# Sample queries first, projections in quarter chunks, and prompt values in plain float32 on four column quarters

## The chip, the cores and the metric

The kernel runs on one core of one Trainium2 chip. The metric is the device time of one execution in microseconds. Three runs of the kernel before gave 2160.17, 2162.57 and 2163.04 us, a median of 2162.57 us. A separate execution was taken with the hardware profiler; its own time was 2163.56 us, of which its trace spans 2161.8 us.

## The reference, cut to what matters

One decoder layer is computed for 1024 prompt tokens and 32 sample tokens (8 sequences of 4 tokens with 2048 cached positions each), all in float32:

```
x = x + 0.5 * swiglu(rms_norm(x), w1, w3, w2)          # FFN 1
p = rms_norm(x) @ w_in                                  # q, k, v, forget logits, B gate, C gate, conv input
logf = log_sigmoid(fl + b_f);  uc = cg * u
o = softmax(q.k / 8 + sum of logf between key and query, causal) . v     # 8 heads of 64
      # prompt: 1024 keys of its own;  sample: 2048 cached keys by page table + its 4 new ones
conv = bg * conv3(uc)                                   # 512 channels, causal, width 3
x = x + concat(rms_norm(o), rms_norm(conv)) @ w_out
x = x + 0.5 * swiglu(rms_norm(x), w1', w3', w2')        # FFN 2
y = rms_norm(x)
```

Outputs are y for prompt and sample, and the new k, v, logf and conv state.

## The kernel before, in words

Activations stand with channels on the partitions and the 1056 tokens along the free side. A float32 product is mostly made of three matmuls in the rounded type `fp32r`: weight and activation are each split into a high and a low part (ScalarE casts the high part, line 86, VectorE subtracts for the low part, line 88), and `mm3` (lines 101 to 105) adds high x high, high x low and low x high. A few products (transposes, sample attention, some of the prompt's values) use plain float32 matmuls; the trace records each of these as two matmul instructions.

The order of instructions on each engine is not simply the order of the program. A planner goes over the whole program at compile time, with its own estimates of durations and with the program order as priority, and fixes an order for each engine and each DMA queue. On the chip every engine then runs its list strictly in order, and waits at an instruction whose input is late.

The stages in time are FFN 1 up and down (to about 741 us), the mixer (741 to 1147 us: all projections by `w_in`, and the whole attention of the sample tokens), the attention of the prompt (1147 to 1309 us), the output projection `w_out` (to about 1420 us), and FFN 2.

*Mixer, lines 570 to 982.* `w_in` is used in 24 column blocks of 128 (4 each of q, k, v, B gate, C gate, conv input). `proj`, `values` and `conv` load one block (512 KB, line 78, on SP's queue), split it, and compute it for three chunks of 352 tokens; `win` (line 612) makes one chunk, 8 x 3 matmuls, in one of three PSUM buffers `pg`. The prompt's q and k are written to memory as high and low parts (line 648), k also as an output (line 644), v twice (lines 961, 962); all of these go through SP's queue. `forget` (line 656) computes the forget gates and their running sums. The attention of the sample tokens, `sample(g)` for two groups of four sequences, is a generator. It first scans the cached forget gates (VectorE, line 823), which `load_gates` gathers page by page through the POOL queue (line 599; 16 gathers per group, by a table `idl` that 16 small DMAs of line 462 fill). Then it takes 16 chunks of keys (1 MB each: two pages on SP's queue, line 781, two on POOL's, line 599, into a ring of four buffers `kvraw`) for the scores (line 832), does the softmax, transposes it (line 859), and takes 16 chunks of values (line 874). Its products have 32 output rows per head pair, and use the array as four column quarters of 32 at the same time. In program order the four q blocks come first, whole; then k, values and conv run chunk by chunk, and after each chunk the sample generator is stepped at 1.2, 0.9 and 1.5 steps per chunk (lines 972 to 982).

*Attention of the prompt, lines 991 to 1128.* It runs over 8 heads x 8 query blocks of 128. `logits` computes scores (lines 1049, 1050, 1052), maximum, exponential and scaled probabilities `Pr`; it runs LA = 3 blocks ahead. `flip` transposes `Pr` by TensorE (line 1069) and copies it out of PSUM. `weigh` multiplies with the values for a pair of query blocks, PVD = 4 blocks behind. Even heads split probabilities and values into high and low parts: two `fp32r` matmuls of 256 columns per key block j (lines 1089, 1090), after a copy on ScalarE (line 1073) and a subtraction on VectorE (line 1075). Odd heads (`NATIVE`) use one plain float32 matmul of 64 rows by 256 columns per j (line 1085). A query block pair m needs 2m + 2 key blocks, of which the last has 128 columns: 20 per head. Two of the four chunks of the conv norm are placed after blocks 28 and 60 (`CONV_AT`). The loads of `w_out` are tied behind the loads of head 6 (`K.after`, line 1038).

Of the kernel before, what the change touches and what calls it, by code (L numbers as in the profile page):

```python
# [18 lines left out]
P = 128  # L19
# [8 lines left out]
H = 8  # L28
# [11 lines left out]
NATIVE = (1, 3, 5, 7)  # L40
LA, PVD, PTB, PRB = 3, 4, 3, 4
CONV_AT = (28, 60)
RK, RV, RC = 1.2, 0.9, 1.5
# [384 lines left out]
def kernel(ctx: ExitStack, tc: tile.TileContext, io: dict):  # L428
# [141 lines left out]
    with ExitStack() as es:  # L570
# [85 lines left out]
        def forget(other):  # L656
# [8 lines left out]
            for c in range(NMC):  # L665
                if c == NMC - 1:

                    other()
# [7 lines left out]
                nc.vector.tensor_add(z[:H, cs], ps[32:32 + H], z[:H, cs])  # L676
            zt = mix.tile([P, 9, H], F32, name="zt")
# [27 lines left out]
            nc.sync.dma_start(io["fo"][SEQ:TOK, :], lf[:NS, 8, :])  # L705
            LF = mix.tile([P, TOK], F32, tag="U", bufs=1, name="LF")
# [10 lines left out]
            T2 = smp.tile([P, PAST + P], F32, tag="B", bufs=1, name="T2")  # L717
# [19 lines left out]
            for t in range(1, NT):  # L737
# [3 lines left out]
                                  cst[:H, C_SELH:C_SELH + P].rearrange("h (b a c) -> h a b c", a=NHP, c=8))  # L741
            pcn = ptr.tile([P, 512], F32, tag="tr", name="pcn")[:, :NS]
# [45 lines left out]
        new = []  # L788
# [24 lines left out]
        def sample(g):  # L813

            if g == 0:
                load_gates(0)
            S = smp.tile([P, PAST + P], F32, tag="S", bufs=1, name="S")
            nc.gpsimd.memset(S[:, PAST + NS:], NEG)
            B = smp.tile([P, PAST + P], F32, tag="B", bufs=1, name="B")
            nc.vector.memset(B[:, 0:1], 0.0)  # L820
# [30 lines left out]
            if g == 0:  # L851
                load_gates(1)
# [11 lines left out]
            while not new:  # L864
                yield
# [469 lines left out]
```

## Time and profile before

| | us |
|---|---|
| runs, median of 3 | 2162.57 |
| profiled execution, its own time | 2163.56 |
| its span | 2161.8 |
| mixer stage, 741 to 1147 us | 406 |
| prompt attention, 1147 to 1309 us | 162 |

In the rows below, PE is TensorE's matmul, PEld its weight load, DVE is VectorE, ACT ScalarE, POOL GpSimd, SP SyncE (whose queue issues most DMAs). `L103` is line 103 of the kernel. A matmul's recorded duration overlaps the next matmul, so the time that one takes is read from start to start.

### The profile page before, as it was taken

What the parts mean: (1) busy time and instruction counts of PE and PEld (TensorE: products, weight loads), DVE (VectorE), ACT (ScalarE), POOL (GpSimd) and SP (SyncE); (2) the same over time, 40 slices, a digit from 0 to 9 for tenths busy, and PEclk for the clock granted to TensorE, in tenths of its full rate; (3) what the DMA queues carried; (4) which work ended last, traced back from release to release, by engine and by line L of the source; (5) the groups of instructions that cost most, each with busy time, mean ns of one, the idle gap of its engine ahead of it and who ended that gap; (6) DMA issues with size and microseconds to landing.
All of it is one profiled execution on the core that took longest, in us unless ns stands there. A gap on an engine that the chain in (4) does not pass through costs nothing. (4 is left out here: it accounts for less than half of the span.)

```text
span 2161.8 us, 42854 instructions
## 1 busy us (share of the span) xinstructions
PE 2098.5 (97%) x16738; PEld 1995.7 (92%) x16738; DVE 1352.4 (63%) x2604; ACT 876.1 (41%) x1754; POOL 264.3 (12%) x367
## 2 busy tenths in 40 slices
PE   7999999999999989999898999999999999999998
PEld 7999999999999877897697777999999999999997
DVE  8877777776656742322226785897677677775354
ACT  6533333344434422211115774453333333454343
POOL 0010001110000054234340000001010101100000
PEclk9999999999999989999998999999999999999999
DMA  6222222247546549869886436432222222496353
GB/s 212 77 93 91 84 85 93 93 162 238 198 139 212 167 150 329 297 201 312 253 262 142 111 95 201 144 107 88 76 80 73 86 85 84 142 311 210 108 180 131
DMA packets 138795, 335.15 MB, mean 155 GB/s; under 512 B 28144, under 2 KB 47568, under 8 KB 137056
## 3 DMA queue, kind: packets, MB, share of 16 engines
q1 hardware_dynamic: 116736, 263.66, 38.6%
q0 software_dynamic: 21856, 68.76, 9.1%
q8 instruction: 131, 2.15, 0.4%
q14 instruction: 72, 0.59, 0.1%
HBM read 276.09 MB, written 56.24 MB: 154 GB/s over the span
## 5 line engine op out<-in xcount | busy, mean ns | idle before, releaser
L103 PE MATMUL ps<-op,wh 128*128 128x264 f32 x2604 | 742.2, 285 | 2.9 <-ACT op L192 2.4
L105 PE MATMUL ps<-op,wl 128*128 128x264 f32 x2604 | 744.4, 286 | 0.0
L104 PE MATMUL ps<-op,wh 128*128 128x264 f32 x2604 | 743.1, 286 | 0.0
L86 ACT CAST wh<-wraw 128x512 fp32r<-128x512 f32 x536 | 312.8, 600 | 487.6 <-PE ps L104 281.3
L88 DVE TENSOR_TENSOR wl<-wraw,wh 128x512 fp32r<-128x512 f32 x536 | 347.3, 663 | 250.1 <-ACT wh L86 238.7
L103 PEld LDWEIGHTS ps<-op,wh 128*128 128x128 f32 x2604 | 492.8, 189 | 4.4 <-ACT op L192 2.8
L104 PEld LDWEIGHTS ps<-op,wh 128*128 128x128 f32 x2604 | 491.4, 189 | 0.4 <-DVE op L193 0.2
L105 PEld LDWEIGHTS ps<-op,wl 128*128 128x128 f32 x2604 | 491.5, 189 | 0.2
L103 PE MATMUL ps<-h,wh 128*128 128x264 f32 x1408 | 402.0, 285 | 0.0
L104 PE MATMUL ps<-h,wh 128*128 128x264 f32 x1408 | 400.5, 284 | 0.0
L105 PE MATMUL ps<-h,wl 128*128 128x264 f32 x1408 | 398.1, 283 | 0.5 <-DVE wl L88 0.5
L105 PEld LDWEIGHTS ps<-h,wl 128*128 128x128 f32 x1408 | 264.9, 188 | 0.7 <-DVE wl L88 0.7
L104 PEld LDWEIGHTS ps<-h,wh 128*128 128x128 f32 x1408 | 264.8, 188 | 0.2
L103 PEld LDWEIGHTS ps<-h,wh 128*128 128x128 f32 x1408 | 264.8, 188 | 0.2
L103 PE MATMUL pg<-XH,wh 128*128 128x352 f32 x576 | 196.0, 340 | 8.2 <-DVE zl L631 4.2
L104 PE MATMUL pg<-XL,wh 128*128 128x352 f32 x576 | 190.5, 331 | 0.0
L105 PE MATMUL pg<-XH,wl 128*128 128x352 f32 x576 | 189.7, 329 | 0.0
L86 ACT CAST wh<-s 128x512 fp32r<-128x512 f32 x176 | 107.7, 616 | 115.7 <-PE ps L104 106.9
L103 PEld LDWEIGHTS pg<-XH,wh 128*128 128x128 f32 x576 | 111.6, 194 | 34.7 <-issue 11.9
L88 DVE TENSOR_TENSOR wl<-s,wh 128x512 fp32r<-128x512 f32 x176 | 120.7, 690 | 26.6 <-ACT wh L86 22.5
L326 POOL DMA_DIRECT2D h_d<-t x79 | 42.7, 540 | 598.3 <-DVE t L325 598.3
L104 PEld LDWEIGHTS pg<-XL,wh 128*128 128x128 f32 x576 | 111.8, 194 | 0.0
(274 smaller groups left out, 2610.5 us busy)
## 6 DMA issues: line engine op xcount, KB each, us to landing
wraw<-in_w2a SPq DMA_DIRECT2D x48, 512.0 KB
wraw<-in_w2b SPq DMA_DIRECT2D x48, 512.0 KB
h_d<-t POOLq DMA_DIRECT2D x176, 132.0 KB, 2.0
h<-h_d SPq DMA_DIRECT2D x88, 264.0 KB
kvraw<-in_kc SPq DMA_DIRECT2D x64, 256.0 KB
kvraw<-in_vc SPq DMA_DIRECT2D x64, 256.0 KB
wraw<-in_w1a SPq DMA_DIRECT2D x28, 512.0 KB
wraw<-in_w3a SPq DMA_DIRECT2D x28, 512.0 KB
```

The lines of the kernel that those rows point to most:

```text
L86: nc.scalar.copy(wh, x)
L88: nc.vector.tensor_sub(wl, x, wh)
L103: nc.tensor.matmul(ps, w[0], x[0], start=start, stop=False)
L104: nc.tensor.matmul(ps, w[0], x[1], start=False, stop=False)
L105: nc.tensor.matmul(ps, w[1], x[0], start=False, stop=stop)
L326: nc.gpsimd.dma_start(h_d[2 * p + 1][:, f, :], t)
```

## The change

- `win` yields after each quarter of a chunk (two of the eight channel blocks, six matmuls), so that work of the sample attention can come between quarters.
- The mixer's order becomes: gathers of the first group's forget gates; forget gates, q block 0 whole, and of q blocks 1 to 3 only the last chunk (which holds the sample tokens); then k, values, the other two chunks of q blocks 1 to 3 (their weights are loaded and split a second time), and conv, in quarters. Beside these the sample generator takes two steps whenever 0.27 steps per quarter have added up to two. There are 264 quarters and 70 steps.
- The sample attention takes keys of both groups first, then values of both. The scan of the gates is written into the score buffer itself; the second buffer `B` is gone, `kvraw` has five buffers in place of four, and the transposed probabilities two in place of one.
- In the prompt's attention all heads use plain float32: `weigh` makes, per key block and query block, two matmuls of 32 rows by 128 columns, so that two query blocks fill the four column quarters. The splits of probabilities and values go; `flip` of odd heads copies on VectorE from the fifth key block on. `PVD` becomes 2, the result has one PSUM buffer, the conv norm has a PSUM buffer of its own and comes after blocks 20 and 44, and the tie of the `w_out` loads is gone.

```diff
-NATIVE = (1, 3, 5, 7)
-LA, PVD, PTB, PRB = 3, 4, 3, 4
-CONV_AT = (28, 60)
-RK, RV, RC = 1.2, 0.9, 1.5
+LA, PVD, PTB, PRB = 3, 2, 5, 4
+RA = 0.27
+CONV_AT = (20, 44)
...
-        def win(ws, c, m=P):
-            ps = pg.tile([P, 512], F32, tag="pg", name="pg")[:m, :MC]
+        def win(ws, c):
+
+            ps = pg.tile([P, 512], F32, tag="pg", name="pg")[:, :MC]
             cs = slice(c * MC, (c + 1) * MC)
-            K.dot(ps, ws, [(XH[:, k, cs], XL[:, k, cs]) for k in range(KD)])
+            for k in range(0, KD, 2):
+                K.dot(ps, ws[k:k + 2], [(XH[:, i, cs], XL[:, i, cs]) for i in (k, k + 1)], k == 0, k == KD - 2)
+                if k < KD - 2:
+                    yield
             return ps
...
-        def proj(i, kind, t):
+        def proj(i, kind, t, chunks=range(NMC)):
 
             ws = K.weight(io["w_in"][i], D)
-            for c in range(NMC):
-                ps = win(ws, c)
+            for c in chunks:
+                ps = yield from win(ws, c)
...
-        def forget(other):
+        def forget():
...
-                    other()
+                    yield
...
-            T2 = smp.tile([P, PAST + P], F32, tag="B", bufs=1, name="T2")
+            T2 = smp.tile([P, PAGES + 1, P], F32, tag="PT", bufs=2, name="T2").rearrange("p s r -> p (s r)")
...
-        qs = [proj(t, "q", t) for t in range(NHP)]
-        forget(lambda: next(qs[0]))
-        for g in qs:
-            for _ in g:
-                pass
...
             chunks += [(io["kc"], 4 * g + b, j) for j in range(4) for b in range(4)]
+        for g in range(2):
             chunks += [(io["vc"], 4 * g + b, j) for b in range(4) for j in range(4)]
...
-            raw = smp.tile([P, 4, 512], F32, tag="kvraw", bufs=4, name="kvraw")
+            raw = smp.tile([P, 4, 512], F32, tag="kvraw", bufs=5, name="kvraw")
...
-        def sample(g):
-
-            if g == 0:
-                load_gates(0)
+        PTs, sums = {}, {}
+
+        def sample_keys(g):
+
             S = smp.tile([P, PAST + P], F32, tag="S", bufs=1, name="S")
             nc.gpsimd.memset(S[:, PAST + NS:], NEG)
-            B = smp.tile([P, PAST + P], F32, tag="B", bufs=1, name="B")
-            nc.vector.memset(B[:, 0:1], 0.0)
+            nc.vector.memset(S[:, 0:1], 0.0)
...
-                nc.vector.scalar_tensor_tensor(S[:, ks], ps, cq[:, g:g + 1], B[:, ks], ALU.add, ALU.add)
+                nc.vector.scalar_tensor_tensor(S[:, ks], ps, cq[:, g:g + 1], S[:, ks], ALU.add, ALU.add)
                 yield
             pn = ptr.tile([P, 512], F32, tag="tr", name="pn")[:, :NS]
+            if g == 0:
+                load_gates(1)
+            while not keys:
+                yield
...
             nc.scalar.activation(S, S, AF.Exp, bias=nm, accum_out=sm)
             nc.vector.reciprocal(sm, sm)
-            if g == 0:
-                load_gates(1)
+            sums[g] = sm
             yield
-            PT = smp.tile([P, PAGES + 1, P], F32, tag="PT", bufs=1, name="PT")
+            PT = PTs[g] = smp.tile([P, PAGES + 1, P], F32, tag="PT", bufs=2, name="PT")
...
+        def sample_values(g):
+            PT = PTs[g]
...
-        A = chain(sample(0), sample(1))
+        def k_proj():
+            for t in range(NHP):
+                yield from proj(NHP + t, "k", t)
+            keys.append(True)
+
+        def q_rest():
+            for t in range(1, NHP):
+                yield from proj(t, "q", t, range(NMC - 1))
+
+        def take(g_, n):
+            for _ in range(n):
+                next(g_, None)
+
+
+        load_gates(0)
+        gate = forget()
+        q0 = proj(0, "q", 0)
+        next(gate)
+        take(q0, 8)
+        next(gate)
+        take(q0, 5)
+        next(gate)
+        for t in range(1, NHP):
+            take(proj(t, "q", t, (NMC - 1,)), 5)
+            next(gate, None)
+        A = chain(sample_keys(0), sample_keys(1), sample_values(0), sample_values(1))
         due = 0.0
-        for work, rate in ((chain(*(proj(NHP + t, "k", t) for t in range(NHP))), RK),
-                           (values(), RV), (conv(), RC)):
-            for _ in work:
-                due += rate
-                while due >= 1:
-                    next(A, None)
-                    due -= 1
+        for _ in chain(k_proj(), values(), q_rest(), conv(range(4))):
+            due += RA
+            if due >= 2:
+                take(A, 2)
+                due -= 2
...
-            V = ap_.tile([P, 8, 2, HD], F32R, tag="V", bufs=2, name="V")
-            VF = ap_.tile([P, 8, HD], F32, tag="VF", bufs=2, name="VF")
+            V = ap_.tile([P, 8, P], F32, tag="V", bufs=2, name="V")
             for j0 in range(0, 8, 4):
                 pt_ = ptr.tile([P, 512], F32, tag="tr", bufs=2, name="ptv")
                 for j in range(4):
                     nc.tensor.transpose(pt_[:, j * P:(j + 1) * P],
                                         vt[:, (j0 + j) * P:(j0 + j + 1) * P], ident)
-                pv_ = pt_.rearrange("p (j a d) -> p j a d", j=4, a=2)
-                nc.scalar.copy(V[:, j0:j0 + 4, 0, :], pv_[:, :, 0, :])
-                nc.vector.tensor_sub(V[:, j0:j0 + 4, 1, :], pv_[:, :, 0, :], V[:, j0:j0 + 4, 0, :])
-                nc.scalar.copy(VF[:, j0:j0 + 4, :], pv_[:, :, 1, :])
-            return V, VF
+                nc.scalar.copy(V[:, j0:j0 + 4].rearrange("p j d -> p (j d)"), pt_)
+            return V
...
-                ins = nc.sync.dma_start(dst.bitcast(F32), src)
-            if h == 6:
-                K.after = ins.ins
+                nc.sync.dma_start(dst.bitcast(F32), src)
...
-                pv_ = pt_[:, :n * P].rearrange("p (j q) -> p j q", q=P)
-                hi = pt2[0][:, j0:j0 + n, c0:c0 + P]
-                nc.scalar.copy(hi, pv_)
-                if h not in NATIVE:
-                    nc.vector.tensor_sub(pt2[1][:, j0:j0 + n, c0:c0 + P], pv_, hi)
+                copy = nc.vector.tensor_copy if h % 2 and j0 else nc.scalar.copy
+                copy(pt[:, j0:j0 + n].rearrange("p j q -> p (j q)"), pt_[:, :n * P])
 
         def weigh(h, m, pt2):
-            V, VF = vs[h // 2]
-            pr = slice(HD * (h % 2), HD * (h % 2) + HD)
-            O = ppv.tile([P, 512], F32, tag="pv", bufs=2, name="O")
-            nj = 2 * m + 2
-            for j in range(nj):
-                c0 = P if j == nj - 1 else 0
-                if h in NATIVE:
-                    nc.tensor.matmul(O[:HD, c0:256], VF[:, j, :], pt2[0][:, j, c0:], start=j == 0,
-                                     stop=j == nj - 1)
-                else:
-                    w = V[:, j].rearrange("p c d -> p (c d)")
-                    nc.tensor.matmul(O[:, c0:256], w, pt2[0][:, j, c0:], start=j == 0, stop=False)
-                    nc.tensor.matmul(O[:, c0:256], w, pt2[1][:, j, c0:], start=False, stop=j == nj - 1)
+
+            V, vc = vs[h // 2], slice(HD * (h % 2), HD * (h % 2) + HD)
+            O = ppv.tile([P, 512], F32, tag="pv", bufs=1, name="O")[:, :P]
+            c0 = vc.start
+            for j in range(2 * m + 2):
+                for b, pt in enumerate(pt2):
+                    n = 2 * m + b
+                    for q in range(0, HD if j <= n else 0, 32):
+                        nc.tensor.matmul(O[HD * b + q:HD * b + q + 32], V[:, j, c0 + q:c0 + q + 32],
+                                         pt[:, j, :], start=j == 0, stop=j == n)
             at = ap_.tile([P, 256], F32, tag="at", bufs=3, name="at")
-            if h in NATIVE:
-                nc.scalar.copy(at[pr], O[:HD, :256])
-            else:
-                nc.scalar.copy(at[pr], O[HD:, :256])
-                nc.vector.tensor_add(at[pr], O[:HD, :256], at[pr])
-            nc.sync.dma_start(at_d[h // 2][pr, 256 * m:256 * m + 256], at[pr])
+            nc.scalar.copy(at[vc, :P], O[:HD])
+            nc.vector.tensor_copy(at[vc, P:], O[HD:])
+            nc.sync.dma_start(at_d[h // 2][vc, 256 * m:256 * m + 256], at[vc])
...
+            pts[n] = ap_.tile([P, 8, P], F32, tag="PT", bufs=PTB, name="PT")
+            flip(h, i, prs.pop(n), pts[n])
+            behind(n - PVD)
             if n in CONV_AT:
-                conv_norm(n == CONV_AT[1], ap_.tile([P, 4, CH], F32, tag="co", bufs=1, name="co"),
-                          ppv.tile([P, 512], F32, tag="pv", bufs=2, name="pco")[:, :CH])
+                conv_norm(CONV_AT.index(n), ap_.tile([P, 4, CH], F32, tag="co", bufs=1, name="co"),
+                          pco.tile([P, 512], F32, tag="pco", bufs=1, name="pco")[:, :CH])
```

`behind(k)` calls `weigh` for an odd block k with the transposed probabilities of blocks k - 1 and k. `forget` has five yields, after each of which the main program goes on with q; `conv` and `values` take their chunks with `yield from win(ws, c)`.

## Rows read from the trace of the kernel before

**Rows 1.** The page's busy time of each engine over the whole span.
```profile
PE 2098.5 (97%) x16738; PEld 1995.7 (92%) x16738; DVE 1352.4 (63%) x2604; ACT 876.1 (41%) x1754; POOL 264.3 (12%) x367
```
**Rows 2.** Stages: window, length, busy and instructions by engine, clock, DMA share, GB/s.
```profile
741.00:1147.00 406.00, 382.77 (x3204) 332.78 (x3203) 113.63 (x235) 81.76 (x167) 159.74 (x171) 0.96 0.78 248
1147.00:1309.00 162.00, 152.99 (x917) 113.73 (x918) 124.32 (x278) 117.16 (x289) 0.61 (x2) 0.96 0.44 109
1309.00:1420.00 111.00, 106.06 (x773) 100.74 (x773) 83.35 (x139) 52.11 (x88) 3.20 (x6) 0.95 0.55 185
```
**Rows 3.** TensorE in time order, mixer, value steps: start, duration, instruction, [idle before].
```profile
960.57 0.32 PE L105 MATMUL pg<-XH,wl 128*128 128x352 f32 x1
960.81 1.08 PE L874 MATMUL pv<-kvraw,PT 128*32 128x128 f32 x32
961.83 0.43 PE L103 MATMUL pg<-XH,wh 128*128 128x352 f32 x1
...
965.61 0.32 PE L105 MATMUL pg<-XH,wl 128*128 128x352 f32 x1
965.87 1.08 PE L874 MATMUL pv<-kvraw,PT 128*32 128x128 f32 x32
966.76 0.40 PE L879 MATMUL pv<-VS,PT 128*32 128x128 f32 x8
966.98 1.06 PE L874 MATMUL pv<-kvraw,PT 128*32 128x128 f32 x32
967.97 0.43 PE L103 MATMUL pg<-XH,wh 128*128 128x352 f32 x1
```
**Rows 4.** TensorE in time order, mixer, two key steps in a row.
```profile
875.43 0.32 PE L105 MATMUL pg<-XH,wl 128*128 128x352 f32 x1
875.68 1.93 PE L832 MATMUL sc<-kvraw,QZ 128*32 128x512 f32 x16
877.53 0.43 PE L103 MATMUL pg<-XH,wh 128*128 128x352 f32 x1
```
**Rows 5.** Groups by line and shape: counts, busy us, mean ns, idle before.
```profile
L103 PE MATMUL pg<-XH,wh 128*128 128x352 f32 x576 | 196.0, 340 | 8.2 <-DVE zl L631 4.2 <-ACT QZ L637 4.0
...
L832 PE MATMUL sc<-kvraw,QZ 128*32 128x512 f32 x256 | 35.2, 618 | 10.2 <-DMA kvraw<-in_kc 8.0 <-ACT QZ L637 2.2
...
L874 PE MATMUL pv<-kvraw,PT 128*32 128x128 f32 x1024 | 33.9, 275 | 2.7 <-DMA kvraw<-in_vc 2.0 <-DMA kvraw<-in_vc,idx 0.7
```
**Rows 6.** TensorE in time order, mixer, the three longest idle times.
```profile
783.20 0.66 PE L103 MATMUL pg<-XH,wh 128*128 128x352 f32 x1 [4.21 <-DVE zl L631]
...
797.91 0.66 PE L103 MATMUL pg<-XH,wh 128*128 128x352 f32 x1 [4.02 <-ACT QZ L637]
...
1046.90 1.93 PE L832 MATMUL sc<-kvraw,QZ 128*32 128x512 f32 x8 [8.01 <-DMA kvraw<-in_kc]
```
**Rows 7.** VectorE in time order: first and last of four gate scans.
```profile
781.45 1.28 DVE L823 TENSOR_TENSOR_SCAN B<-ones,B,R 128x512 f32<-128x512 f32 x1 [1.22 <-DMA R<-in_lf,idl]
...
795.62 1.28 DVE L823 TENSOR_TENSOR_SCAN B<-ones,B,R 128x511 f32<-128x511 f32 x1 [3.73 <-DMA R<-in_lf,idl]
```
**Rows 8.** POOL in time order: the first two of 16 gate gathers.
```profile
772.87 1.08 POOL L599 DMA_INDIRECT R<-in_lf,idl  x1 [10.54 <-DMA out_fo<-lf]
774.26 1.00 POOL L599 DMA_INDIRECT R<-in_lf,idl  x1 [0.30 <-issue]
```
**Rows 9.** Waits of SP's queue, 1000 to 1050 us: total, times, longest.
```profile
SPq L910 <- DMA out_cso<-E: 9.7, 1, 9.7
```
**Rows 10.** A stretch of the k projections, columns as in Rows 2.
```profile
845.00:865.00 20.00, 20.00 (x133) 15.71 (x126) 4.93 (x9) 5.12 (x11) 9.72 (x10) 1.00 0.98 356
```
**Rows 11.** TensorE in time order, prompt attention: values of an odd head.
```profile
1193.29 2.16 PE L1085 MATMUL O<-PTh,VF 128*64 128x256 f32 x10
1195.38 0.50 PE L1049 MATMUL S<-KA,QA 128*128 128x512 f32 x1
```
**Rows 12.** TensorE in time order, prompt attention: values of an even head.
```profile
1256.35 0.28 PE L1090 MATMUL O<-PTl,V 128*128 128x256 f32 x1
1256.47 0.23 PE L1089 MATMUL O<-PTh,V 128*128 128x128 f32 x1
1256.53 0.28 PE L1090 MATMUL O<-PTl,V 128*128 128x128 f32 x1
```
**Rows 13.** Waits of the prompt attention: total, times, longest.
```profile
PEld ptp L1069 <- DVE PTl L1075: 2.7, 7, 0.5
```

More of the change, by code (lines that the diff above doesn't have):

```diff
@@ L705, in forget @@
             nc.sync.dma_start(io["fo"][SEQ:TOK, :], lf[:NS, 8, :])
+            yield
             LF = mix.tile([P, TOK], F32, tag="U", bufs=1, name="LF")
@@ L787 @@
         taken = []
-        new = []
+        keys, new = [], []
         def kv_chunk():
@@ L901, in vnew, with conv @@
             new.append(VS)
-        def conv():
-            for t in range(4):
+        def conv(ts):
+            for t in ts:
                 q = nc.gpsimd if t == 3 else nc.sync
@@ L913, in conv @@
                 for c in range(NMC):
-                    ps = win(ws, c)
+                    ps = yield from win(ws, c)
                     g_ = mix.tile([P, MC], F32, tag="cg", bufs=3, name="cg")
@@ L920, in conv @@
                 for c in range(NMC):
-                    ps = win(ws, c)
+                    ps = yield from win(ws, c)
                     cs, n = cols(c)
@@ L946, in conv @@
                 for c in range(NMC):
-                    ps = win(ws, c)
+                    ps = yield from win(ws, c)
                     st = mix.tile([P, MC], F32, tag="st", bufs=3, name="st")
@@ L956, in values @@
                 for c in range(NMC):
-                    ps = win(ws, c)
+                    ps = yield from win(ws, c)
                     cs, n = cols(c)
@@ L992 @@
         ap_ = pool(es, "ap", "left")
+        mix = pool(es, "mixb", "left")
+        pco = pool(es, "pco", space=PSUM)
         ptr = pool(es, "ptr2", space=PSUM)
@@ L1099 @@
         qk, vs, prs, pts = {}, {}, {}, {}
-        blocks = [(h, 2 * m + j) for h in range(H) for m in range(4) for j in range(2)]
-        qk[0] = load_qk(0)
+        blocks = [(h, i) for h in range(H) for i in range(8)]
         def ahead(n):
@@ L1106, in ahead, with behind @@
                 prs[n] = logits(h, i)
-                if n % 8 == 0 and h + 1 < H:
+                if i == 0 and h + 1 < H:
                     qk[h + 1] = load_qk(h + 1)
-                if n % 8 == 2 and h % 2 == 0:
+                if i == 2 and h % 2 == 0:
                     vs[h // 2] = load_v(h // 2)
+        def behind(k):
+            if k >= 0 and k % 2:
+                h, i = blocks[k]
+                weigh(h, i // 2, [pts.pop(k - 1), pts.pop(k)])
+        qk[0] = load_qk(0)
         for n in range(LA):
@@ L1115 @@
             ahead(n + LA)
-            if i % 2 == 0:
-                pts[h, i // 2] = [ap_.tile([P, 8, 256], F32 if h in NATIVE else F32R, tag=t, bufs=PTB, name=t)
-                                  for t in ("PTh", "PTl")[:1 if h in NATIVE else 2]]
-            flip(h, i, prs.pop(n), pts[h, i // 2])
-            k = n - PVD
-            if k >= 0 and k % 2:
-                weigh(blocks[k][0], blocks[k][1] // 2, pts.pop((blocks[k][0], blocks[k][1] // 2)))
+            pts[n] = ap_.tile([P, 8, P], F32, tag="PT", bufs=PTB, name="PT")
+            flip(h, i, prs.pop(n), pts[n])
+            behind(n - PVD)
             if n in CONV_AT:
-                conv_norm(n == CONV_AT[1], ap_.tile([P, 4, CH], F32, tag="co", bufs=1, name="co"),
-                          ppv.tile([P, 512], F32, tag="pv", bufs=2, name="pco")[:, :CH])
+                conv_norm(CONV_AT.index(n), ap_.tile([P, 4, CH], F32, tag="co", bufs=1, name="co"),
+                          pco.tile([P, 512], F32, tag="pco", bufs=1, name="pco")[:, :CH])
         for k in range(len(blocks) - PVD, len(blocks)):
-            if k % 2:
-                weigh(blocks[k][0], blocks[k][1] // 2, pts.pop((blocks[k][0], blocks[k][1] // 2)))
+            behind(k)
     es_ps = ctx.enter_context(ExitStack())
```

11 lines of the change are left out of this document (6 added, 5 removed).

## The prediction

> **What bounds the kernel now.** I first read the page's busy times: TensorE is busy 97% of the span, no other engine above 63% [rows 1]. So what counts is how many matmuls there are, what each takes from start to start, and where TensorE stands still or runs slowly. The table by stage shows where the latter is: in the mixer the weight loads fill only 333 of 406 us and the mean clock is 0.96, in the prompt's attention 114 of 162 us [rows 2]. Then the timeline inside these two stages for the price of each kind of matmul, and the waits in it for what stops TensorE.
>
> In the mixer a projection matmul takes 0.16 us: 23 of them between 961.83 and 965.61, the first one longer after the change of kind [rows 3]. The 24 column blocks of `w_in` make 24 x 3 x 24 = 1728 (a third of them is the x576 of [rows 5]), 276.5 us; the forget gates' 48 make 7.7. A value step of the sample attention, alone between two chunks, takes 960.73 to 961.83, 1.10 us. Two in a row, with eight more matmul records of 0.22 (966.76 to 966.98), take 965.77 to 967.97, 2.20, so 1.98 without them [rows 3]. Two key steps in a row take 875.59 to 877.53, 1.94 us [rows 4]. So a step costs 0.88, and going into and out of column quarters 0.22 each time. In pairs, 32 key steps are 31.0 and 32 value steps 31.7 us, plus 8 x 0.22 for the new tokens. The two sets of 17 transposes and the small products of gates, softmax and results I put at 9, the start at half clock at 2: together 360 us. The stage lasts 406. **46 us of it are no work of TensorE's.** The three longest idle times are 4.2, 4.0 and 8.0 us [rows 6]; after each the matmuls are longer than 0.32 us, the lower clock. A mean of 0.96 between levels of 1.0 and 0.5 is 8% of the stage, some 32 us, at 1.2 GHz. Idle time and slow clock overlap in part; with the single steps below they make up nearly all of the 46.
>
> Where the idle times come from: the first two stand behind VectorE's `zl` and what follows it. VectorE runs in order, and four scans of the forget gates are ahead of `zl` on it; each waits for its gathers, the last until 795.62 [rows 7]. The gathers begin at 772.87, 16 of them at about 1.3 us [rows 8]. The third is a late chunk of keys; SP's queue, which loads half of each chunk, stood 9.7 us at one small load (line 910) that waited for an 8-byte-grained store of the same buffer [rows 9].
>
> **The change in the mixer.** It removes no matmul and adds none. By the code the old rates give about 12, 11 and 36 places where steps come in (59), the new one 35 pairs: 24 x 0.22 = 5.3 us gone. The q blocks 1 to 3 are loaded and split twice: 3 more loads of 512 KB on SP's queue, six more casts on ScalarE, six more subtractions on VectorE. These engines are busy 82 and 114 us of 406 [rows 2], so I cost them at nothing; without that cover it would be one block's cast and subtraction, about 2.5 us, each time. That is most likely in the start, where q blocks 1 to 3 need a new block every 3.8 us.
>
> *Gates.* `load_gates(0)` moves ahead of everything in the program, but its gathers wait for the table `idl`, whose loads were already first. I expect the gathers at 773 to 794 as before. TensorE does forget, q block 0 and three last chunks, (48 + 6 x 24) x 0.16 = 31 us, plus small products, and is at k by about 777. VectorE is then still behind the scans, and k's `zl`, with its stores and the loads queued behind those on SP, waits for it. Three `pg` buffers hold 11.5 us of TensorE's work, and scans alternate with other work, so part is hidden. Of some 16 us lost there (two idle times of 8.2 and the slow clock that follows) I keep 8; bounds 0 and 16.
>
> *Late chunks.* With 35 pairs over 264 quarters a pair comes every 7.4 x 0.96 + 1.96 = 9.1 us and takes 2 MB. The fifth `kvraw` buffer lets a chunk's load start when the one five before it is done; before, it was four, at 1.5 steps per chunk. The time between is then about 18 us instead of 11, which covers most of a 9.7 us stop of SP's queue. I keep 4 of the 11 us (8.0 and the slow matmuls after it); bounds 0 and 11. The stage moved 248 GB/s x 406 us = 100.7 MB; with 1.6 MB more in 376 us that is 272 GB/s. [Rows 10] show 356 GB/s at a DMA share of 0.98 with TensorE busy all 20 us, so it fits on average; for k, with three stores per chunk, it is near the limit, and I allow 4 us.
>
> Sum: 360 + 8 + 4 + 4 = 376, **30 us less than 406**; bounds 46 less (no stall left) and 5 less (only the pairing counts).
>
> **The change in the prompt's attention.** An odd head takes 0.209 us per record of 256 columns (ten from 1193.29 to 1195.38) [rows 11]. With 16 key blocks of 256 and 4 of 128 columns, two records each, that is 32 x 0.209 + 8 x 0.105 = 7.5 us. An even head takes 0.12 per matmul of 256 and 0.06 per 128 [rows 12]: 32 x 0.12 + 8 x 0.06 = 4.3. Four of each: 47.4 us. The new product has exactly the shape of the sample's line 879, four plain float32 matmuls of 128 x 32 by 128 columns on four quarters: 0.22 us per key block [rows 3]. 8 x 20 x 0.22 = 35.2 us, so 12.2 less. The last key block of a pair fills two quarters only and is counted in full.
>
> Around it: going in and out of quarters costs 0.22 per unbroken run [rows 3]. There are 32 products, and the planner cuts some; I take 40 runs, 8.8 us (bounds 7 and 14). The odd heads' half-array mode pays such a price now; I give it the same 0.22, for 16 products cut into perhaps 22 runs, 5 us. The even heads' transposes wait 2.7 us for the subtraction [rows 13], and TensorE's entry into their runs is not free; together 4. So 12.2 + 5 + 4 - 8.8 = **12 us less**; bounds 0 and 19. VectorE and ScalarE are busy 124 and 117 of 162 us [rows 2]. The subtractions leave VectorE and about as much ScalarE work stays, so neither reaches the shorter stage. If they did, the stage would stay near 160. The single PSUM buffer of the result must be copied out before the next product, more than 4 us later: nothing. The earlier conv norms and the untied `w_out` loads I take as zero, within 2 us either way: `w_out`'s stage is TensorE's again [rows 2].
>
> The Trainium skill, TensorEngine Tiling (Array Packing), Key Properties, says that changing the tiling mode, not just the tile, drains TensorE. The trace agrees with 0.22 us per run. By that rule a planner that cuts each of the 32 products into four runs would take 28 us for them and the stage would gain nothing, which is the second rival below.
>
> **Sum.** 2163.6 (the profiled execution's own time; span 2161.8) - 30 - 12 = 2121.6; the runs' median is 1 us below that execution, so 2120.
>
> **Rivals.** (1) *The mixer keeps its stalls.* The gathers start no earlier, the planner sets the scans where it sets them now, and SP stands at line 910 as before. For it: no edit touches `idl` or line 910. Against: the ring is longer and the sample's start later. Mixer 5 less, attention 12: 2163.6 - 17 - 1 = 2146. (2) *The attention gains nothing*, by cut runs or because ScalarE, 72% busy now, sets the pace. 2163.6 - 30 - 1 = 2133. (3) *Slower: chunks late at every pair.* Two chunks are taken at once, and the program asks for loads only up to four chunks ahead, so the second chunk of the next pair is asked for one period, 9.1 us, ahead. If SP's queue, which now also carries the stores of all quarters' chunks, holds those loads, every pair waits and the clock falls after it. The point from which it decides is 42 / 35 = 1.2 us per pair; at 1.5 us the time is 2120 + 52 = 2172. Against it: [rows 10], where chunks came at 1.2 per projection chunk and 356 GB/s with no wait. (4) *It doesn't do what it says*: the planner undoes the new order and cuts the runs, (1) and (2) together, 2163.6 - 5 - 1 = 2158, which is no change.
>
> **How the numbers follow.** Forecast 0.60 (its own range 2104 to 2136), rival (1) 0.20, (2) 0.12, (3) 0.05, (4) 0.03. Both upper bounds give 2163.6 - 46 - 19 - 1 = 2098; the range is 2100 to 2148, which leaves out (3), (4) and the edges. A measurement of this kernel can tell 0.2%, 4 us, from no change: faster 0.92, the same 0.03, slower 0.05.
>
> **What would show it.** In the profile after: a mixer of 370 to 385 us with 35 groups of paired steps; VectorE's scans again waiting for gathers until about 795, but TensorE's idle times there shorter; no idle time of 8 us for keys. The prompt's attention is 150 us, with quarter matmuls at 0.22 per key block in about 40 runs, and ScalarE below 80% of it. Wrong would be a mixer above 395 us, idle times before many pairs, or an attention above 158 us.

## The result, and the profile after

The changed kernel took 2178.49 us (median of 4 runs, 2176.51 to 2180.79) where the kernel before took 2162.76 us beside it: a ratio of 1.0076, 95% interval 1.0058 to 1.0093. It is slower by 16 us; 42 us less had been forecast. The profiled execution took 2176.51 us, its trace spans 2174.8, 13.0 more than before.

TensorE's busy time fell, from the 2098.5 us of [rows 1] to 2082.3. The page's busy times of the kernel after:

```profile
PE 2082.3 (96%) x17570; PEld 1987.5 (91%) x17570; DVE 1344.5 (62%) x2586; ACT 874.5 (40%) x1738; POOL 265.8 (12%) x367
```

The table by stage of the kernel after, columns as in [rows 2]: the mixer, the passage to the prompt's attention, and that attention.

```profile
745.00:1160.00 415.00, 378.87 (x3198) 331.06 (x3197) 118.36 (x235) 87.60 (x176) 159.05 (x166) 0.94 0.76 245
1160.00:1174.00 14.00, 1.01 (x8) 0.79 (x6) 1.81 (x9) 0.00 (x0) 2.66 (x5) 0.67 0.95 256
1174.00:1327.00 153.00, 142.15 (x1748) 108.18 (x1748) 111.67 (x252) 107.48 (x265) 0.00 (x0) 0.94 0.45 107
```

From first to last matmul of each stage, before and after: mixer 405.6 and 415.9, standstill between mixer and first logits 0.6 and 13.0, attention 160.7 and 152.8, all behind it 853.5 and 848.3; the mixer starts 3.3 us later. That is +10.3 + 12.4 - 7.9 - 5.2 + 3.3 = 12.9. Only the first three are put down to the change. The stages outside are the same code, and their differences are of the size that executions differ by: in the later profiles below, of either kernel, the mixer starts between 740.9 and 746.3, and what is behind the attention takes 848.2 to 853.2.

**The passage.** First the kernel before, one row of TensorE and one of SP's queue.

```profile
1147.61 0.49 PE L1049 MATMUL S<-KA,QA 128*128 128x128 f32 x2 [0.62 <-DVE st L949]
```
```profile
1127.32 1.17 SPq L1036 DMA_DIRECT2D KA<-k_d  x1
```

Then the kernel after: TensorE, SP's queue in time order, and two of SP's waits from 1140 to 1165 us (total, times, longest). The brackets name the idle time before an instruction and what ended it; a duration on SP with x3 covers the waits between three issues.

```profile
1159.88 0.32 PE L104 MATMUL pg<-XH,wl 128*128 128x352 f32 x1
1160.04 0.60 PE L892 MATMUL po<-cst,M 128*128 128x128 f32 x4
1173.63 0.77 PE L1074 MATMUL S<-KA,QA 128*128 128x128 f32 x2 [12.99 <-DMA QA<-q_d]
```
```profile
1143.60 16.24 SPq L77 DMA_DIRECT2D wraw<-in_w_out  x3
1160.23 0.80 SPq L1181 DMA_DIRECT2D x<-x_d  x2
1161.09 1.15 SPq L1063 DMA_DIRECT2D KA<-k_d  x2
```
```profile
SPq L77 <- DVE wl L87: 21.4, 3, 13.6
SPq L1181 <- PE pg L104: 0.3, 1, 0.3
```

Head 0's q and k, which the kernel before asked for at 1127 us, are asked for at 1161. Ahead of them on SP now stand three loads of `w_out`, the last held to 1159.5 by a weight buffer that is not free (13.6 us for VectorE's split, line 87), and two loads of x. These wait for a projection matmul (line 104) and go out at 1160.23, just as the mixer's last one ends (1159.88 + 0.32 = 1160.20).

**The mixer.** TensorE's idle times over 1 us there, kernel after, 795 to 905 us (2.6 us at 779.5 and 1.5 us at 906.7 lie outside; behind that there is none):

```profile
801.03 0.25 PE L847 MATMUL pn<-KS,QN 128*32 128x32 f32 x2 [3.27 <-DVE KS L649]
805.11 1.94 PE L832 MATMUL sc<-kvraw,QZ 128*32 128x512 f32 x8 [3.84 <-DMA kvraw<-in_kc]
816.13 1.93 PE L832 MATMUL sc<-kvraw,QZ 128*32 128x512 f32 x8 [9.09 <-DMA kvraw<-in_kc,idx]
822.06 1.94 PE L832 MATMUL sc<-kvraw,QZ 128*32 128x512 f32 x8 [3.99 <-issue]
825.46 1.94 PE L832 MATMUL sc<-kvraw,QZ 128*32 128x512 f32 x8 [1.46 <-DMA kvraw<-in_kc,idx]
...
847.05 1.52 PE L832 MATMUL sc<-kvraw,QZ 128*32 128x512 f32 x2 [3.50 <-DMA kvraw<-in_kc]
849.70 0.66 PE L102 MATMUL pg<-XH,wh 128*128 128x352 f32 x1 [1.13 <-ACT wh L85]
...
886.06 0.66 PE L102 MATMUL pg<-XH,wh 128*128 128x352 f32 x1 [4.99 <-ACT wh L85]
```

The waits of [rows 6] are gone, and more of the same size stand at the first key steps. The sum of idle times in the mixer rose from 23.0 to 36.1 us. In the table of 790 to 850 us, before and after, TensorE's columns say what follows the waits: 182 matmuls instead of 309, at a mean clock of 0.75 instead of 0.91:

```profile
790.00:850.00 60.00, 53.79 (x309) 46.41 (x311) 14.32 (x24) 13.26 (x36) 33.78 (x36) 0.91 0.87 280
```
```profile
790.00:850.00 60.00, 33.72 (x182) 21.32 (x181) 11.31 (x18) 6.79 (x14) 44.62 (x47) 0.75 0.79 261
```

The fifth busy column is GpSimd, 44.6 of 60 us after. Its queue in time order, kernel after: the gate gathers R of group 1 stand between the key gathers that TensorE waits for, each 1.25 us from start to start.

```profile
797.88 0.95 POOL L598 DMA_INDIRECT kvraw<-in_kc,idx  x1 [0.30 <-issue]
799.13 0.95 POOL L598 DMA_INDIRECT kvraw<-in_kc,idx  x1 [0.30 <-issue]
...
800.43 1.29 POOL L598 DMA_INDIRECT R<-in_lf,idl  x1 [0.16 <-issue]
...
807.01 0.94 POOL L598 DMA_INDIRECT R<-in_lf,idl  x1 [0.30 <-issue]
808.26 0.95 POOL L598 DMA_INDIRECT kvraw<-in_kc,idx  x1 [0.30 <-issue]
...
829.63 0.94 POOL L598 DMA_INDIRECT R<-in_lf,idl  x1 [0.30 <-issue]
```

They stood there in the kernel before as well, from 794.25 to 821.4 us, and its first six key gathers among them came within 3 us of the changed kernel's. But its first key step started only at 819.55 us, where the changed kernel's starts at 792.63. GpSimd's queue, kernel before:

```profile
794.25 0.95 POOL L599 DMA_INDIRECT R<-in_lf,idl  x1 [0.16 <-DMA R<-in_lf,idl]
795.51 0.95 POOL L599 DMA_INDIRECT kvraw<-in_kc,idx  x1 [0.30 <-issue]
...
809.25 0.95 POOL L599 DMA_INDIRECT kvraw<-in_kc,idx  x1 [0.30 <-issue]
...
820.50 0.94 POOL L599 DMA_INDIRECT R<-in_lf,idl  x1 [0.30 <-issue]
```

VectorE, kernel after: the last gate scan of group 0 waits for its gather, and the copy KS behind it is what TensorE waits for at 801.03.

```profile
799.18 1.28 DVE L823 TENSOR_TENSOR_SCAN S<-ones,S,R 128x511 f32<-128x511 f32 x1 [3.72 <-DMA R<-in_lf,idl]
...
800.80 0.17 DVE L649 COPY KS<-st 128x32 f32<-128x32 f32 x1
```

So the theories were: **A**, the untied loads of `w_out` hold SP ahead of head 0; against it **B**, the loads of x do that. **C**, the mixer's own start is short of keys, by GpSimd's queue (C1) or because the sample begins too soon (C3); against it, bandwidth and SP's queue (C2), or a disturbance from `w_out` (D).

### The profile page after: what moved, and what is told of

Its sections match the earlier page's. It is cut to its first block, busy times and chain, and to the rows that moved or that the text cites. A ratio compares the mean times of both kernels' runs of the same rounds, so it can differ in the third digit from the quotient of the medians.

```text
span 2174.8 us, 44542 instructions
## 1 busy us (share of the span) xinstructions
PE 2082.3 (96%) x17570; PEld 1987.5 (91%) x17570; DVE 1344.5 (62%) x2586; ACT 874.5 (40%) x1738; POOL 265.8 (12%) x367
## 4 chain that ended last, share of the span: by engine, by line
PE 90%; DMA 4%; DVE 2%; ACT 1%; issue 1%; SPq 1%; POOL 1%; DVEq 0%; ACTq 0%; POOLq 0%
PE ps L104 23%; PE ps L103 23%; PE ps L102 23%; PE pg L102 4%; PE pg L103 4%; PE pg L104 4%; PE O L1107 2%; PE ptp L1093 1%; PE pv L880 1%; DMA wraw<-in_w_in 1%; PE sc L832 1%; PE S L1074 1%; PE ps L141 1%; PE S L1075 1%; DMA wraw<-in_w_out 1%
## 5 line engine op out<-in xcount | busy, mean ns | idle before, releaser
L85 ACT CAST wh<-wraw 128x512 fp32r<-128x512 f32 x542 | 317.3, 600 | 497.2 <-PE ps L103 283.1
L104 PEld LDWEIGHTS pg<-XH,wl 128*128 128x128 f32 x576 | 110.1, 191 | 0.9 <-DVE sm L854 0.8
```

What stands on the lines that cost most here:

```text
L85: nc.scalar.copy(wh, x)
L104: nc.tensor.matmul(ps, w[1], x[0], start=False, stop=stop)
```

## The experiments

The kernels with one chip number ran on one chip, beside the kernel before. That kernel's median was 2187, 2187, 2170 and 2166 us on chips II to V, so a kernel is compared by its ratio to it. Stage times are of one profiled execution, as above; "stand" is the standstill before the first logits. On chips II and III the mixers also hold 8 to 34 us of slow stretches, described in the last section, which differ from profile to profile of the same code; mixers of these two chips are therefore not compared with each other.

| run | chip | ratio | 95% interval | mixer | stand | attention |
|---|---|---|---|---|---|---|
| changed kernel | first | 1.0076 | 1.0058-1.0093 | 415.9 | 13.0 | 152.8 |
| e1_tie | II | 1.0038 | 1.0022-1.0053 | 441.1 | 10.3 | 156.8 |
| e1x_tie_x | II | 0.9986 | 0.9972-1.0001 | 428.6 | 0.2 | 151.8 |
| e2_attn_only | II | 1.0017 | 1.0004-1.0030 | 424.3 | 10.6 | 154.4 |
| e3_mixer_only | II | 1.0024 | 1.0010-1.0038 | 436.1 | 0.2 | 162.4 |
| after_again | III | 1.0039 | 1.0023-1.0055 | 433.1 | 11.0 | 153.0 |
| g1 | III | 0.9957 | 0.9940-0.9974 | 431.0 | 0.2 | 152.5 |
| d1 | III | 0.9950 | 0.9928-0.9972 | 427.4 | 0.2 | 151.4 |
| gd | III | 0.9902 | 0.9881-0.9923 | 414.9 | 0.2 | 153.3 |
| before_again | IV | - | - | 409.5 | 0.6 | 163.1 |
| x_only | IV | 1.0015 | 1.0001-1.0029 | 417.9 | 7.2 | 155.5 |
| nogates | IV | 0.9928 | 0.9903-0.9954 | 403.2 | 0.2 | 152.5 |
| gd2 | IV | 0.9918 | 0.9899-0.9938 | 399.1 | 0.2 | 154.8 |
| gd2_again | V | 0.9905 | 0.9890-0.9920 | 404.9 | 0.2 | 151.5 |
| pw | V | 0.9880 | 0.9864-0.9895 | 389.5 | 0.2 | 152.0 |
| ng2 | V | 0.9880 | 0.9861-0.9899 | 391.8 | 0.2 | 154.9 |
| la4 | V | 0.9901 | 0.9885-0.9916 | 398.8 | 0.2 | 149.5 |

**The passage: three ties.** e1_tie puts the tie of `w_out` back, x_only ties the loads of x instead, e1x_tie_x does both.

```diff
-                nc.sync.dma_start(dst.bitcast(F32), src)
+                ins = nc.sync.dma_start(dst.bitcast(F32), src)
+            if h == 6:
+                K.after = ins.ins            # e1_tie: the loads of w_out wait for this place
...
-                nc.sync.dma_start(xs[c][i], x_d[c][:, 4 * i:4 * i + 4, :])
+                with tc.issue_after(K.after) if K.after else nullcontext():   # e1x_tie_x
+                    nc.sync.dma_start(xs[c][i], x_d[c][:, 4 * i:4 * i + 4, :])
```

> The changed kernel with one edit undone: the loads of `w_out` are again queued behind the loads of head 6. Theory A (the removed tie): in the changed kernel three `w_out` loads stand ahead of head 0's q and k loads on SP and wait until 1159.5 us for a free weight buffer, so TensorE stands 13.0 us at the first logits. With the tie the stand goes to about 1 us and the time from 2178.5 to about 2166 us. Rival B: the two loads of x from scratch (1160.23 us in the changed kernel), which are now early too, hold SP as long by themselves, since their memory is only free when the mixer's last matmul is done. Then the stand stays at 10 to 13 us and the time at 2175 to 2179 us.

> The same, and the loads of x for the output projection are queued behind head 6's loads too. Theories A and B both expect the stand at the first logits gone (under 2 us) and a time of 2164 to 2167 us; if neither queue order is the cause, but the memory of head 0's tiles, it stays at 2178 us with head 0's loads still issued after 1160 us.

> The changed kernel with only the loads of x tied behind head 6's loads; `w_out`'s loads stay untied. Together with the run of both ties (0.9986) and of `w_out`'s tie alone (1.0038) this completes the square. If either of the two loads holds SP's queue by itself, head 0's loads are late here too: TensorE stands 8 to 13 us at the first logits, ratio 1.003 to 1.004. If only the loads of x mattered, the stand is under 2 us and the ratio 0.999.

SP's queue and TensorE's first logits with the tie of `w_out` alone:

```profile
1183.45 0.81 SPq L1183 DMA_DIRECT2D x<-x_d  x2
1184.35 1.15 SPq L1063 DMA_DIRECT2D KA<-k_d  x2
```
```profile
1194.13 0.77 PE L1076 MATMUL S<-KA,QA 128*128 128x128 f32 x2 [10.27 <-DMA QA<-q_d]
```
```profile
SPq L1183 <- PE pg L104: 23.0, 1, 23.0
```

The last projection matmul begins at 1183.10 and lasts 0.32: the loads of x go out 0.03 us after its end, and SP stood 23.0 us for it. A alone falls. With the loads of x tied but `w_out` free, head 0 is late by 7.2 us:

```profile
1147.16 16.24 SPq L77 DMA_DIRECT2D wraw<-in_w_out  x3
1163.50 1.15 SPq L1063 DMA_DIRECT2D KA<-k_d  x2
```
```profile
1171.42 0.76 PE L1076 MATMUL S<-KA,QA 128*128 128x128 f32 x2 [7.22 <-DMA QA<-q_d]
```

So either of the two holds the queue by itself, and the two do not add: 10.3 and 7.2 us alone, 11.0 to 13.0 together. With both tied:

```profile
1147.49 1.15 SPq L1063 DMA_DIRECT2D KA<-k_d  x2
```
```profile
1171.03 0.50 PE L1076 MATMUL S<-KA,QA 128*128 128x128 f32 x2 [0.18 <-DVE st L955]
```

The stand is gone, and with it 0.0052 of the time, 11 us, against e1_tie on the same chip.

**The two halves of the change.** e2_attn_only and e3_mixer_only join one half of the changed kernel, cut at the end of the mixer, to the other half of the kernel before, with its constants and its tie.

> The kernel before with the new prompt attention alone (plain float32 values in four column quarters, with its buffers and places of the conv norms), the old mixer, and the tie of the `w_out` loads kept. From the changed kernel's trace the attention costs 152.8 instead of 160.7 us. If that belongs to the attention, the time is 2162.8 - 8 = 2155 us. If the loads of x get ahead of head 0's loads here too (theory B above), 10 to 12 us of that are lost and the time is 2165 to 2167 us.

> The kernel before with the new mixer alone, the old attention and the tie of the `w_out` loads kept. Theory C (the mixer itself got slower, since its sample steps now begin while GpSimd's queue is full of gate gathers and chunks of keys come late): mixer 415 instead of 405 us, time 2162.8 + 10 = 2173 us. Rival D (the mixer only looks longer in the changed kernel because its last casts and loads of `w_out` disturb it): mixer 395 to 405 us, time 2153 to 2163 us.

e2 is the second of its two cases: the attention gains, and the loads of x take it back. They are early with the old mixer too, so what moves them belongs to the new attention; SP's queue in e2_attn_only:

```profile
1167.18 0.81 SPq L1153 DMA_DIRECT2D x<-x_d  x2
1168.08 1.15 SPq L1033 DMA_DIRECT2D KA<-k_d  x2
```

Why they are early is argued, not shown: the new attention's buffers are smaller, so x's tiles may no longer lie in memory that the attention uses, and the planner may place their loads as soon as it expects the mixer to end. e3 is 1.0024, 5 us slower, and shows no stand: the mixer's loss is its own (C), and D falls. Its size here is half of the 10 us on the first chip.

**The measure.** after_again is the changed kernel unaltered.

> The changed kernel once more, unaltered, on this chip, as the measure for the three others. On the first chip it was 1.0076 of the kernel before, on the chip of the earlier runs the two parts alone were 1.0017 and 1.0024. If the parts add up wherever they run, it is 1.004 here; if the stalls of the mixer's start depend on the chip, it is 1.008 again where the chip is like the first.

The parts add: 0.0017 + 0.0024 = 0.0041, measured 0.0039. The larger 0.0076 of the first chip did not return; why is not shown.

**The mixer's start.** g1 queues group 1's gate gathers behind chunk 15's key gathers, d1 starts the pairs later, gd and gd2 do both; all with both ties.

```diff
-                    gather(R[:, s, :], io["lf"], idl[:, g, col:col + 1])
+                    with tc.issue_after(lasts[15].ins) if g else nullcontext():   # g1, gd, gd2
+                        gather(R[:, s, :], io["lf"], idl[:, g, col:col + 1])
...
-RA = 0.27
+RA = 0.285          # d1, gd;  gd2: 0.30
-        due = 0.0
+        due = -4.0  # d1, gd;  gd2: -8.0
```

> The changed kernel with `w_out`'s and x's loads tied behind head 6 (as in the run before, 0.9986 of the kernel before) and the 16 gate gathers of sample group 1 queued behind the key gathers of chunk 15 on GpSimd, so that no gate gather of group 1 stands between key gathers. Theory C1 (GpSimd's queue starves the first key steps: 32 gate gathers of 1.25 us and the key gathers): the waits of TensorE for key gathers between 800 and 850 us go, 10 to 15 us, ratio about 0.993. Rival C2 (the weight and key loads on SP or the DMA engines themselves set the pace there): ratio 0.998 to 1.000, the mixer as long as without the edit.

> The same ties as in g1, the gate gathers where they were, but the sample's first pair comes two pair periods (about 16 us) later and the pairs then a little denser (0.285 instead of 0.27 steps per quarter chunk). Theory C3 (the sample begins before its keys can be there, whoever brings them): the waits before 850 us go, 10 to 15 us, ratio 0.992 to 0.994. Under C1 the group 1 gate gathers still stand between key gathers, and at most half of that is gained; if the bandwidth of the first 100 us is the limit, nothing, 0.998.

> Both edits of g1 and d1. If C1 and C3 are two names of one shortage, it is as good as the better of the two (0.993); if they add, 0.988 to 0.990. If neither does anything, 0.998.

> As the run with both ties, group 1's gate gathers behind chunk 15's and the later first pair (0.9902), with the first pair two periods later still (about 30 us after the changed kernel's) and 0.30 steps per quarter chunk. If the shortage of the first 100 us is not over by then, it gains once more, 0.986 to 0.988; if it is over, the denser pairs give as much back, 0.990 to 0.992.

Against the ties alone (0.9986, another chip) g1 gives 0.29% and d1 0.36%, less than either theory asked, and both together 0.84%: within the intervals they add, as gd's expectation put it for two causes. By mixer g1 gains almost nothing against after_again (431.0 and 433.1), which was rival C2's sign; but its profile holds 20 us of the slow stretches and after_again's 8, so the ratio decides. The stretch from 790 to 850 us, first after_again, then gd, shows it in the first busy column, the clock and GpSimd (fifth):

```profile
790.00:850.00 60.00, 32.10 (x143) 21.14 (x145) 9.89 (x14) 5.82 (x12) 36.84 (x39) 0.72 0.66 199
```
```profile
790.00:850.00 60.00, 48.47 (x254) 36.06 (x253) 11.20 (x19) 9.08 (x19) 27.33 (x29) 0.80 0.80 264
```

TensorE does 254 matmuls instead of 143 there, with fewer gathers beside it (the slow stretches of the last section take 6 and 9 us of the two windows, so they do not make the difference). A still later start (gd2, on two other chips) moved nothing more that can be told: 0.9918 and, repeated, 0.9905, against 0.9902.

**No gate gathers.** In nogates and ng2 one memset per R tile stands in for the gathers, so the gates' part of the sample is left out; ng2 also has gd2's late start.

```diff
-                    gather(R[:, s, :], io["lf"], idl[:, g, col:col + 1])
+                nc.gpsimd.memset(R.rearrange("p s k -> p (s k)"), 0.0)
```

> The changed kernel with both ties, without the 32 gate gathers (each R tile is filled with zeros by one memset; the gates' part of the sample is left out). Theory C1 (the gate gathers on GpSimd keep the sample's first keys late): the mixer loses 20 us or more against the run with both ties (428.6 us), ratio 0.989 or less. Rival C2 (the bandwidth and SP's queue set the pace of the first 100 us): 5 us, ratio 0.996 to 0.999.

> Both ties, no gate gathers at all (zeros in R; the gates' part of the sample is left out), the latest first pair. If the gate gathers are still what keeps the mixer long after both edits, the mixer is 385 us or less and the ratio 0.986 or less. If the gathers no longer matter once they and the pairs are moved, it equals the run with them, 0.990 to 0.993.

Between the two theories: all 32 gathers were worth 14.7 us of mixer (417.9 in x_only to 403.2), or 12 us by the ratios (1.0015 to 0.9928, less x_only's stand). That is more than the mixer's loss on this chip (409.5 in before_again to 417.9), so C1 covers the loss; but a mixer without a gate gather is still far from the forecast 376, and in its profile TensorE waits 3.9 and 8.7 us for weights instead. After the late start the gathers are worth 4 us by the medians (2146.31 to 2142.01; the single runs overlap), 13 by the two profiles' mixers.

**What is left.** pw asks for each weight block one block ahead, on top of gd2.

```diff
+        seq = ([0, 1, 2, 3] + list(range(4, 12)) + [1, 2, 3]
+               + [b + t for t in range(4) for b in (16, 20, 12)])
...
-            ws = K.weight(io["w_in"][i], D)
+            ws = win_w(i)    # loads of seq up to the next block, then split of block i
```

> The kernel with both ties, group 1's gate gathers behind chunk 15's and the latest first pair (0.9918 on the chip before), once more as the measure for the other three on this chip: 0.988 to 0.993.

> The same with each block of `w_in` asked for one block ahead in the program, so that it stands ahead of the stores and key loads of the block before it on SP. Theory D1 (what is left of the mixer's stalls is weights that are asked for too late: 9.5 us before 832.5, 2.2 and 2.7 us later, and the slow clock after each): 8 to 14 us less than the run without it, ratio about 0.987. Rival D2 (the transfers take their time wherever they stand on SP, since the DMA engines are 0.8 to 0.95 busy): the wait moves from the weights to the keys, no difference.

TensorE and SP in gd2_again, then SP in pw. A weight load that is asked for at 820.59, behind ten key loads since 799 us, is waited for until 827.97; in pw the same block is asked for at 791.22.

```profile
827.97 0.66 PE L102 MATMUL pg<-XH,wh 128*128 128x352 f32 x1 [9.96 <-ACT wh L85]
```
```profile
820.59 0.43 SPq L77 DMA_DIRECT2D wraw<-in_w_in  x1
```
```profile
791.22 0.45 SPq L77 DMA_DIRECT2D wraw<-in_w_in  x1
```

D1 holds in the main. pw's median is 7 us under gd2_again's (2139.30 and 2146.31, and no run of the one reaches the other's), just less than was expected, and TensorE's idle times in the mixer fall from 26.9 to 18.3 us, with no wait for a weight over 1 us. Two waits for keys of 2.2 and 2.3 us are new; that much went as D2 had it. The mixer of pw:

```profile
742.00:1132.00 390.00, 371.58 (x3203) 330.03 (x3203) 116.21 (x234) 85.25 (x173) 159.10 (x166) 0.98 0.82 262
```

At 0.9880 of the kernel before (0.9864 to 0.9895) pw beats both kernels: 27 us under the one, and 34 to 42 us under the other (0.9880 against 1.0039 and 1.0076).

**The attention's lookahead.** la4 is gd2 with `LA` 4 and `PRB` 5.

> The first of these four with the prompt attention's logits four blocks ahead instead of three (and five buffers of weights instead of four). In the changed kernel TensorE waits 4.6 to 6.1 us of the attention for ScalarE's exponentials. If it is the lookahead, these go and the attention is 149 us instead of 153, ratio 0.002 lower. If ScalarE's queue order is the cause, it stays within 1 us.

The attention took 149.5 instead of gd2_again's 151.5 us, the number that the first case named, but not by its mechanism: the waits for the exponentials stayed (6.1 us, then 6.2). They were not the lookahead's. What went are other waits, of the transposes for a copy and for the values' load; all waits of the stage fell from 12.2 to 7.7 us. The ratios cannot be told apart.

**The chip.** before_again is the kernel before, profiled.

> The kernel before, unaltered, profiled on a later chip, where it takes about 2187 instead of 2163 us. In the changed kernels profiled there TensorE has stretches around 794 to 829 us in which matmuls that wait for nothing start 0.7 to 2.8 us apart. If that belongs to the chip, the kernel before shows 10 to 25 us of it too and its mixer is about 430 us; if it belongs to the change, its mixer is 405 us and the 24 us stand elsewhere.

This run met a chip with 2170 us, on which neither it nor the changed kernels show such stretches, so the question stays open for the chips of 2187 us. There they appear with the old mixer too (e2: 16.7 us of idle time between 808 and 828).

## Why the prediction was wrong

*"... the untied `w_out` loads I take as zero, within 2 us either way: `w_out`'s stage is TensorE's again."* This step failed by 12 us. It asked what the loads are worth where they are used, not what they would stand in front of. In the kernel before the tie kept them behind head 6; without it the planner put them ahead of head 0's loads on SP, at an instruction that waits for a buffer. And it did not see that the new attention would let the loads of x move up to the same place; either kind of load is enough by itself (e1_tie, x_only). The slower kernel that the prediction did allow for, chunks late at every pair, is not this one.

*"Of some 16 us lost there ... I keep 8"; "I keep 4 of the 11 us"; "it fits on average".* Most facts under these were right: group 0's gate gathers run from 775.11 to 798 and the last scan starts at 799.18, the late chunk of 1046 is gone, and TensorE waits nowhere over 1 us behind 907 although SP's queue still stands once for 10.6 and once for 5.6 us. What failed is the inference that less would be lost at the start. The first key step moved from 819.55 to 792.63 us while the gathers stayed, so keys were wanted while GpSimd's queue was full. One reading was wrong as well: the prediction counts 16 gathers, to 794 us, but in the trace of the kernel before the 16 of group 1 follow at once, to 821 us. The diff moves `load_gates(1)` ahead of group 0's softmax, but that is not what put them there; they run from 794.25 to 821.4 before and from 800.43 to 830.6 after. So g1 does not undo an edit of the diff: it clears a queue that was as full before, when nobody waited for it. An average of bandwidth over 376 us says nothing on the first 60.

In the terms of the sum, the step's mixer of 376 = 360 + 8 + 4 + 4 is 415.9: TensorE's instructions, from start to start without idle times, take 379.8 us instead of 360, and the idle times 36.1 instead of 16 (before: 382.6 and 23.0). Much of the 20 us above 360 is the lower clock: the key steps alone take 38.9 us, not 31.0. Moving the gathers and the first pair, and asking for weights earlier, brought the mixer to 389.5, on another chip. Of the remaining 13.5 us idle times make 2 (18.3 against 16) and TensorE's instructions 11 (371.3 against 360), most of it 77 projection matmuls that still take 0.28 us instead of 0.16.

*35 pairs.* TensorE turns to the sample's key and value steps 33 times in the kernel after, but 47 times before, not 59: the planner had joined some. So 14 x 0.22 = 3.1 us instead of 5.3.

*The attention, -12.* Measured 7.9, inside its bounds, but in part by luck: the terms were off in both directions. Groups of the prompt's attention in the kernel after, by line: busy time and mean ns, then idle time before and its causes.

```profile
L1107 PE MATMUL O<-PT,V 128*32 128x128 f32 x1152 | 48.6, 281 | 1.2 <-DVE at L1111 1.1
L1093 PE MATMUL ptp<-cst,Pr 128*128 128x128 f32 x288 | 48.3, 285 | 2.9 <-ACT PT L1096 2.1 <-DVE PT L1096 0.8
L1074 PE MATMUL S<-KA,QA 128*128 128x512 f32 (+2 forms) x96 | 40.5, 424 | 17.6 <-DMA QA<-q_d 13.0 <-ACT Pr L1082 4.6
```

From start to start, idle times taken out, the value products went from 61.3 to 45.7 us, a gain of 15.6. The new cost was met: 35.2 + 8.8 = 44.0 was forecast, and there are 48 unbroken runs instead of 40, at (45.7 - 35.2) / 48 = 0.22 us, the price of [rows 3]. (The drain of which the Trainium skill speaks, TensorEngine Tiling (Array Packing), Key Properties, agrees with both; the four runs per product by which it could have taken the whole gain did not come, 48 for 32 products.) The old one was 9 us higher than the 47.4 + 5 put: the odd heads took 35.7, as put, but the even heads 25.5 instead of 17.3, because the first and last matmuls of their 34 runs take longer than the 0.12 read inside one run. The prediction had put this entry into the runs, and the transposes' waits for the subtraction, at 4 together. The transposes came out as a loss: in 80 runs instead of 71 they went from 33.8 to 36.8, and all waits in the stage from 7.6 to 10.8, the one for the exponentials from 2.9 to 4.6.

The signs that the prediction named decided it: a mixer above 395 us was to prove it wrong, and did; idle times "before many pairs" were not seen, only before the first few.

## What to carry to other kernels

A tie on a queue is costed by what would stand in front if it went: list the loads that a planner may move up, and ask what each waits for; an edit elsewhere (here the attention's) can free such a load just as an edit to it can. Before work is started earlier, look at the queue that feeds it in that very stretch, not at a mean over the stage, and count every gather that stands in it there: a queue that is full costs nothing until someone waits for it. When one wait is removed, the next comes up behind it: here the gathers, then the first pair, then the weights, each worth 6 to 8 us.

## What the runs showed of the hardware

The kernel before took 2163 to 2187 us from one chip to another. On the two chips of 2187 us TensorE had stretches of up to 34 us in which projection matmuls that waited for nothing in the trace started 0.7 to 2.8 us apart, in multiples of about 0.70 us; such matmuls make 8 to 34 us of each profile there (after_again the least, e3_mixer_only the most) and none of the others. TensorE in e3_mixer_only, where all of one chunk's 24 matmuls took from 793.53 to 827.33 us ([rows 3] show 3.8 us), at a mean granted clock of 0.56 (the lower level is 0.5), though the first of them still ran at the upper one:

```profile
810.49 0.45 PE L104 MATMUL pg<-XL,wh 128*128 128x352 f32 x1 [1.65 <-issue]
811.89 0.45 PE L105 MATMUL pg<-XH,wl 128*128 128x352 f32 x1 [0.94 <-issue]
814.00 0.45 PE L103 MATMUL pg<-XH,wh 128*128 128x352 f32 x1 [1.66 <-issue]
816.79 0.45 PE L104 MATMUL pg<-XL,wh 128*128 128x352 f32 x1 [2.33 <-issue]
```

They lie beside GpSimd's gathers (busy 22.0 of these 33.8 us), while SP's queue issues nothing from 793.6 to 827.1; what causes them was not found.
